# A hybrid attention layer on one core: attention steps of a tile spread over a slot and a half, with part of their elementwise work on GpSimd

## The chip, the cores and the metric

The kernel runs on one core of one Trainium2 chip. The metric is the device time of one execution in microseconds (us). Each core has a tensor engine (PE; PEld is its weight load), a vector engine (DVE), a scalar engine (ACT), GpSimd (POOL) and SyncE (SP), which here only issues DMAs. The engines run their own instruction streams in order and wait for one another through semaphores.

## What is computed

One inference step of one decoder layer: 2048 prompt positions and 8 x 4 sample positions, model width 1024. Its first part, on which the change bears, is cut here to what matters:

```
qa, ka, va, qb, kb, vb, ga, gb = split(x @ w_in)      # 1024 -> 5120
qa, ka, qb, kb = rope(...)
A:  8 query / 2 kv heads, window 128, learned sinks, in 128-blocks
B:  3 groups x 4 heads, (window, dilation) = (128,1), (512,4), (2048,16)
    keys of a block: the block before it and itself, masked to a band
    group 3 has one block per residue, so no block before it
ob = merge of the three groups by their softmax denominators
m  = sigmoid(ga) * (oa @ w_br_a) + sigmoid(gb) * (ob @ w_br_b);  m @ w_o
```

Samples do the same against cached keys and values. A gated ConvFFN and two layer norms follow. All is fp32 in and out; matmuls take each operand as a high part (rounded to the tensor engine's fp32r) and a low part (the rest), so a product takes three matmuls.

## The kernel before

Phase 1 is the input projection with the attention in it; phases 2 and 3 (merge, W_o, ConvFFN) aren't touched. Phase 1 runs in *slots*. A slot takes one tile of 128 rows (M) through the four weight units of its *kind*: B0, B1, B2 (q, k, v of one group and 256 gate columns), A, then G (gates alone). A kind has 16 tiles and, at i == 16, one *sample slot* for the 32 sample rows; the order of tiles is natural for B0 and A, strided by 4 for B1 and by 16 for B2. B1's tiles have a block before them except every fourth, B2's never have.

In a slot (`slot`), each of the four units goes through 8 blocks of k in two halves: 8 *steps* of 12 matmuls of 128x256 (8 of them in a sample slot). I name steps 0 to 7; step 2u + kh is unit u, half kh. After each step the code calls `adv`, which moves each waiting generator of `self.jobs` by one yield: this is where the attention of the tile before is interleaved. Steps also take two pieces of weight splitting for the next kind (`adv_w`, paced) and two times a slot a piece of the sample scores (`adv_bg`). Halves of the projection's output land in two PSUM buffers (`pd`); the first half's `evac` (the rope of q, for B of q and k) is called late, after step 5 in B and step 4 in A, the second half's (v, gate) at the slot's end. After step 1 (units 0 done), `prep` loads the next cos/sin and x and makes the next tile's `xs`: the high part on ACT, the low part on DVE (on GpSimd in A).

`attn_b` of a tile, by steps of the slot after its own: 0 transposes q, splits it, transposes k, splits it; 1 splits v; 2 scores (`qk`) and softmax (`softmax_pair`: per head a fused add-mask and maximum on DVE with its accumulator read, then nm = -scale x maximum on DVE, then the exponential with its sum on ACT); 5 and 6 transpose the two halves of P (`transpose_p`: PE, high part on ACT, low part on DVE); 7 and step 0 of the next slot multiply with the values and add the parts (`both`: ACT copies one half of the partitions, DVE adds; GpSimd adds the two products). `adv` takes the newest job first. `attn_a` has two rounds of scores (r = 0, 1; heads in pairs) whose four pairs' softmax, transposes and values are dealt out over ten steps singly. `sample_scores` multiplies a cached block of keys with broadcast queries (L797) and sums it (L800), both on DVE, in one piece.

PSUM tiles: psS 2 (scores), psT 3 (transposes, second value tile), psO 1 (values). All SBUF scratch of 128x512 comes from one ring of 10 (`buf`).

## Time and profile before

| what | us |
|---|---|
| median of 3 runs | 3261.59 (3256.7 to 3264.81) |
| the profiled execution | 3259.99, its span 3258.2 |
| PE, PEld busy | 3175.0 (97%), 2907.4 (89%) |
| DVE, ACT, POOL busy | 1947.6 (60%), 1397.0 (43%), 565.5 (17%) |
| dense projection matmuls L379 | 1001.1 busy, 7680 of them |
| mean granted PE clock | 0.994 |

PE's time is the sum of its pipelined matmuls as modelled, so that 97% says that it is hardly ever without one, not that it is at its peak. In the timeline a row is a run of alike instructions: its start, how long it lasts from the first's begin to the last's end, and in brackets how long the engine stood idle ahead of it and which instruction released it. Since matmuls overlap, the start of the next row tells more than the length.

### The profile page before, as it was taken

How to read it: one execution, taken by the hardware profiler on the slowest of the kernel's cores; microseconds unless marked ns; L12 is line 12 of the kernel's file. 1: busy time of each engine (PE TensorE's matmuls, PEld its weight loads, DVE VectorE, ACT ScalarE, POOL GpSimd, SP SyncE). 2: the span in 40 equal slices, each digit the busy share in tenths (PEclk: the TensorE clock that was granted, in tenths of full speed). 3: DMA queues.
4: the chain of work that ended last, by engine and by line, in shares of the span. 5: the costliest groups of instructions: out<-in, count | busy, mean ns of one | idle time of the engine just before them, and what ended most of it. 6: DMA issues, size and time to landing. Idle time of an engine off the chain costs nothing.

```text
span 3258.2 us, 56718 instructions
## 1 busy us (share of the span) xinstructions
PE 3175.0 (97%) x21839; PEld 2907.4 (89%) x21839; DVE 1947.6 (60%) x4030; ACT 1397.0 (43%) x3097; POOL 565.5 (17%) x671
## 2 busy tenths in 40 slices
PE   8999999999999899899999999999999999999999
PEld 8998999999899899788877988888888888999998
DVE  5667877877887632577765444564446444574446
ACT  6666656665666533412224243342243332342332
POOL 2112112223121200255540000030002100030001
PEclk9999999999999999999999999999999999999999
DMA  3113212412221343876744323443334423443231
GB/s 116 56 47 95 82 31 86 121 63 89 79 57 38 91 131 98 227 194 175 187 131 140 121 84 101 127 142 91 95 100 120 139 86 101 120 138 91 69 95 57
DMA packets 480036, 343.02 MB, mean 105 GB/s; under 512 B 113938, under 2 KB 435564, under 8 KB 479766
## 3 DMA queue, kind: packets, MB, share of 16 engines
q1 hardware_dynamic: 462390, 290.78, 31.5%
q0 software_dynamic: 17232, 48.56, 4.8%
q8 instruction: 172, 2.82, 0.4%
q14 instruction: 98, 0.80, 0.1%
q10 hardware_dynamic: 144, 0.07, 0.0%
HBM read 279.71 MB, written 59.59 MB: 104 GB/s over the span
## 4 chain that ended last, share of the span: by engine, by line
PE 58%; issue 2%; DMA 2%; DVE 1%; SPq 0%; ACT 0%; POOL 0%; DVEq 0%; POOLq 0%; ACTq 0%
PE psu L1392 31%; PE psdn L1070 14%; PE psw L1070 5%; PE psb L1070 4%; PE psd L379 2%; PE psdf L1070 1%; DMA oa<-d_oa 1%; PE pst L1234 0%; PE pso L964 0%; PE pst L1269 0%; DMA ob<-d_ob 0%; DMA ga<-d_gate 0%; DMA b<-in_w_o 0%; SPq L1126 0%; DMA b<-in_w_br_b 0%
## 5 line engine op out<-in xcount | busy, mean ns | idle before, releaser
L1392 PE MATMUL psu<-h,w 128*128 128x512 f32 (+1 forms) x5280 | 1013.6, 354 | 2.2 <-ACT h L41 2.0
L379 PE MATMUL psd<-w,xs 128*128 128x256 f32 x7680 | 1001.1, 285 | 8.7 <-ACT w L41 4.0
L1392 PEld LDWEIGHTS psu<-h,w 128*128 128x128 f32 x5280 | 861.2, 188 | 149.0 <-ACT h L41 3.4
L379 PEld LDWEIGHTS psd<-w,xs 128*128 128x128 f32 x7680 | 945.7, 190 | 12.9 <-ACT w L41 4.4
L1070 PE MATMUL psdn<-w,gt 128*128 128x256 f32 (+1 forms) x4008 | 474.9, 279 | 2.2 <-DVE y L1443 2.2
L1070 PEld LDWEIGHTS psdn<-w,gt 128*128 128x128 f32 (+1 forms) x4008 | 472.2, 186 | 5.3 <-DVE y L1443 4.5
L42 DVE TENSOR_TENSOR w<-b,w 128x512 fp32r<-128x512 f32 (+1 forms) x613 | 403.7, 717 | 21.4 <-ACT w L41 20.4
L41 ACT ACTIVATE w<-b 128x512 fp32r<-128x512 f32 x636 | 346.5, 607 | 127.4 <-PE psdn L1070 64.2
L1403 ACT ACTIVATE ext<-psu 128x512 f32<-128x512 f32 (+1 forms) x110 | 56.3, 512 | 452.2 <-PE psu L1392 452.1
L1416 DVE SCALAR_TENSOR_TENSOR ac<-ext,cw,ac 128x512 f32<-128x512 f32 (+1 forms) x88 | 71.1, 808 | 286.9 <-ACT ac L1415 286.9
L1443 DVE SCALAR_TENSOR_TENSOR y<-y,psdn 128x256 f32<-128x256 f32 x176 | 73.2, 420 | 274.2 <-PE psdn L1070 270.4
L1070 PE MATMUL psw<-WO,mT 128*128 128x512 f32 (+1 forms) x800 | 189.4, 395 | 0.9 <-DVE mT L42 0.9
L1070 PEld LDWEIGHTS psw<-WO,mT 128*128 128x128 f32 (+1 forms) x800 | 148.5, 186 | 38.9 <-DVE mT L42 1.1
L1412 POOL COPY mix<-ext 128x2 f32<-128x2 f32 x66 | 13.0, 196 | 926.5 <-ACT ext L1403 906.4
L42 DVE TENSOR_TENSOR xs<-R,xs 128x1024 fp32r<-128x1024 f32 x64 | 104.8, 1638 | 114.9 <-ACT xs L41 114.8
L1070 PE MATMUL psb<-w,oT 128*128 128x512 f32 (+1 forms) x600 | 147.6, 404 | 7.7 <-ACT b L449 5.0
L41 ACT ACTIVATE gt<-ac 128x512 fp32r<-128x512 f32 x110 | 58.3, 549 | 222.2 <-DVE ac L1423 162.7
L1070 PEld LDWEIGHTS psb<-w,oT 128*128 128x128 f32 (+1 forms) x600 | 112.4, 190 | 36.3 <-ACT b L449 5.7
L552 ACT ACTIVATE P<-P,nm 128x256 f32<-128x256 f32 (+1 forms) x192 | 86.4, 451 | 123.1 <-issue 87.4
L42 DVE TENSOR_TENSOR PT<-pst,PT 128x512 fp32r<-128x512 f32 (+1 forms) x160 | 96.2, 608 | 66.6 <-ACT PT L41 66.0
L662 POOL TENSOR_TENSOR b<-b 64x256 f32<-64x256 f32 x96 | 71.3, 742 | 337.4 <-DVE b L571 337.4
L41 ACT ACTIVATE xs<-R 128x1024 fp32r<-128x1024 f32 x80 | 116.2, 1452 | 0.9 <-ACT b L756 0.4
(257 smaller groups left out, 3679.1 us busy)
## 6 DMA issues: line engine op xcount, KB each, us to landing
b<-in_w_up SPq DMA_DIRECT2D x352, 256.0 KB, 3.9
b<-in_w_down SPq DMA_DIRECT2D x160, 256.0 KB, 3.4
b<-in_w_in SPq DMA_DIRECT2D x80, 256.0 KB, 4.1
b<-in_x_prompt SPq DMA_DIRECT2D x64, 256.0 KB, 4.0
b<-in_cache_b SPq DMA_DIRECT2D x64, 256.0 KB, 3.3
ga<-d_gate SPq DMA_DIRECT2D x32, 512.0 KB, 5.4
b<-d_q SPq DMA_DIRECT2D x48, 256.0 KB, 3.9
d_gate<-b SPq DMA_DIRECT2D x64, 128.0 KB, 1.9
```

Of the source, the lines that this page charges most:

```text
L41: self.nc.scalar.activation(hi, src, AF.Copy)
L42: (eng or self.nc.vector).tensor_tensor(lo, src, hi.bitcast(F32), ALU.subtract)
L379: nc.tensor.matmul(dst, lhsT=l, rhs=r[:, k, :], start=(k == 0 and q == 0), stop=(k == 7 and q == len(ops) - 1))
L552: nc.scalar.activation(P[:, x, :nk], P[:, x, :nk], AF.Exp, bias=nm[:, c:c + 1], scale=SCALE, accum_out=den[:, c:c + 1])
L662: nc.gpsimd.tensor_tensor(o[:, :, 0], o[:, :, 0], o[:, :, 1], ALU.add)
L1070: self.nc.tensor.matmul(ps[:x.shape[1]], lhsT=x, rhs=w, start=(first and q == 0), stop=(last and q == len(ops) - 1))
L1392: nc.tensor.matmul(ps[:, :b1 - b0], lhsT=w[:, k, c0:c0 + 128], rhs=h[:, x, k, b0:b1], start=(k == 0 and q == 0), stop=(k == 7 and q == 2))
L1403: nc.scalar.activation(ext[:, 2 + b0:2 + e1], ps[:, 0:e1 - b0], AF.Copy)
L1412: nc.gpsimd.tensor_copy(carry[:, j, :], ext[:, W:W + 2])
L1416: nc.vector.scalar_tensor_tensor(ac[:, :L], ext[:, 1:1 + L], cw[:, 1, j:j + 1], ac[:, :L], ALU.mult, ALU.add)
L1443: nc.vector.scalar_tensor_tensor(y[x][:M, cs], y[x][:M, cs], ALPHA if first else 1.0, ps[:M], ALU.mult, ALU.add)
```

## The change

- `adv` takes the oldest job first; what jobs hand to `self.late` runs behind all jobs of that step.
- `prep` runs at the slot's begin, ahead of step 0 (in B0's first slot after step 3). xs's low part goes to GpSimd in B1, B2 and A.
- The first half's rope comes after step 4 in B too. q, k and v of a tile share one buffer `qkv`, so that B's rope of q and k is three instructions of 512 columns and not five.
- `attn_b`: step 0 transposes q and k into one PSUM tile, all high parts ahead of all low ones (`split_qk`); 2 splits v; 3 scores and softmax; then, in the slot after, 0 transposes both halves of P, 2 multiplies both with the values, and `sum_b` adds behind the other jobs of that step.
- `attn_a`: 0 as before with `split_qk`; 3 the first scores; 5 both transposes and the second scores; 7 the first values; in the slot after 0 transposes and 2 values. The output goes out by round, not by kv head (two DMAs a round).
- nm is made on ACT.
- `sample_scores`: the product is made on GpSimd, its sum on DVE one piece later.
- Sample slots (but G's) call `adv` after steps 0, 1, 3 and 7 only.

The core of the diff:

```diff
     def adv(self):
-        for j in self.jobs[::-1]:
+        for j in list(self.jobs):
...
+        while self.late:
+            self.late.pop()()
...
-                        return self.make_xs(nextp[0][2], kind == "A")
+                        return self.make_xs(nextp[0][2], kind != "B0" and kind != "G")
...
-        evac_at = (2, 1) if kind[0] == "B" else (2, 0)
+        evac_at = (2, 0)
...
+        if kind != "B0" or i > 0:
+            out = prep()
         for half in range(2):
...
-                    self.adv()
+                    if not smp or kind == "G" or (u, kh) in ((0, 0), (0, 1), (1, 1), (3, 1)):
+                        self.adv()
...
-                self.rope([(q[:, 0:256].rearrange("p (h d) -> p h d", d=64), 0, 4),
-                           (kv[:, 0:256].rearrange("p (h d) -> p h d", d=64), 4, 8)], ps, cs, 128, 8)
+                self.rope([(t[:, 256:768].rearrange("p (h d) -> p h d", d=64), 0, 8)], ps, cs, 128, 8)
...
-        nc.vector.tensor_scalar(nm[:, csl], m[:, csl], -SCALE, None, ALU.mult)
+        nc.scalar.activation(nm[:, csl], m[:, csl], AF.Copy, scale=-SCALE)
...
+    def split_qk(self, q3, k3, cur):
+        qT, q_lo = self.split_q(q3)
+        k_lo = self.split_k(k3, cur)
+        q_lo()
+        k_lo()
+        return qT
...
         Ps = [self.softmax_pair(sps[x], nk, mask, md[:, 0:4], nm, md[:, 4:8], (x, 2 + x)) for x in range(2)]
         nc.gpsimd.dma_start(self.d_md[g, rows, :], md)
+        for _ in range(5):
+            yield
+        PTs = [self.transpose_p(P, [(c, b) for c in range(2) for b in range(nb)]) for P in Ps]
+        yield
+        yield
...
+        self.late.append(lambda: self.sum_b(g, i, tiles))
...
         sps = scores(0)
+        Ps = [softmax(0, x, sps) for x in range(2)]
         yield
         yield
+        PTs = [trans(P) for P in Ps]
         sps = scores(1)
+        Ps = [softmax(1, x, sps) for x in range(2)]
+        yield
+        yield
+        values(0, PTs)
+        yield
+        PTs = [trans(P) for P in Ps]
+        yield
+        yield
+        values(1, PTs)
...
+            if done is not None:
+                total(*done)
...
-            nc.vector.tensor_tensor(q3, Kv, q3, ALU.mult)
+            nc.gpsimd.tensor_tensor(q3, Kv, q3, ALU.mult)
+            done = (b, th, qb)
```

How this moves instructions shows at three places. PE in a B1 slot before, from the dense steps 2 to 4 on (L379 dense, L562 transposes of P, L659 values, L630 and L634 transposes of q and k of the next tile):

```order
L379 MATMUL psd<-w,xs 128x256 x36
L562 MATMUL pst<-idn,P 128x128 x4
L379 MATMUL psd<-w,xs 128x256 x12
L562 MATMUL pst<-idn,P 128x128 x4
L379 MATMUL psd<-w,xs 128x256 x12
L659 MATMUL pso<-PT,vr 128x256 x4
L379 MATMUL psd<-w,xs 128x256 x12
L630 MATMUL pst<-idn,q 128x128 x2
L634 MATMUL pst<-idn,kv 128x128 x2
L659 MATMUL pso<-PT,vr 128x256 x4
L379 MATMUL psd<-w,xs 128x256 x24
```

and after, from the dense steps 4 to 7 and 0 on (L383 dense, L566 P, L647 q and k, L673 values):

```order
L383 MATMUL psd<-w,xs 128x256 x60
L566 MATMUL pst<-idn,P 128x128 x8
L647 MATMUL pst<-idn,qkv 128x128 x4
L383 MATMUL psd<-w,xs 128x256 x24
L673 MATMUL pso<-PT,vr 128x256 x8
L383 MATMUL psd<-w,xs 128x256 x12
```

Sixty dense matmuls now follow the scores in one run, and two steps stand between P's transposes and the values.

PE in an A slot before, behind the first scores (L619 is their last matmul, L713 values, L562 the transposes of the first pair's P, L617 the second scores):

```order
L619 MATMUL pss<-kL_382,qT 128x256
L713 MATMUL pso<-PT,vr 128x256 x4
L379 MATMUL psd<-w,xs 128x256 x12
L713 MATMUL pso<-PT,vr 128x256 x4
L379 MATMUL psd<-w,xs 128x256 x12
L562 MATMUL pst<-idn,P 128x128 x4
L617 MATMUL pss<-kH_379,qT 128x256
```

and after (L636 the last of the first scores, L634 the first of the second ones):

```order
L636 MATMUL pss<-kL_408,qT 128x256
L383 MATMUL psd<-w,xs 128x256 x24
L566 MATMUL pst<-idn,P 128x128 x8
L634 MATMUL pss<-kH_405,qT 128x256
L634 MATMUL pss<-kH_406,qT 128x256
```

Both pairs' P are now transposed ahead of the second scores; before, the second pair's followed in the next slot.

DVE in the sample slot between B0 and B1 before (L546 maxima of the last tile, L550 nm, L42 lows of the next kind's weights w and of P, L495 the samples' first half):

```order
L546 ISA P,md<-pss,mk 128x256
L546 ISA md 128x1
L550 TENSOR_SCALAR nm<-md 128x2
L42 TENSOR_TENSOR w<-b,w 128x512 x3
L42 TENSOR_TENSOR PT<-pst,PT 128x512
L495 TENSOR_TENSOR b<-psd,b 32x512
```

and after, some instructions later in the same slot (L431 and L438 are the samples' rope, L550 is now the maxima):

```order
L431 TENSOR_TENSOR b<-b,css 32x512
L438 TENSOR_TENSOR sq<-sq,b 32x256
L438 TENSOR_TENSOR b<-b 32x256
L42 TENSOR_TENSOR w<-b,w 128x512 x5
L550 ISA P,md<-pss,mk 128x256
L550 ISA md 128x1
```

The last tile's maxima stood ahead of the weights' lows and now stand behind five of them, and behind them come the samples' second half and six more lows.

More of the change, by code (lines that the diff above doesn't have):

```diff
@@ L219, in phase1 @@
             units += [self.next_unit(pool=True) for _ in range(2)]
-            self.jobs = []
+            self.jobs, self.late = [], []
             self.vprev = None
@@ L388, in slot @@
                         self.adv_bg()
-                if u == (1 if kind[0] == "B" and i == 0 else 0):
+                if u == 1 and kind == "B0" and i == 0:
                     out = prep()
-                    if kind == "G" and i == 14:
-                        rp.close()
-                        self.phase2_weights()
+                if u == 0 and kind == "G" and i == 14:
+                    rp.close()
+                    self.phase2_weights()
                 after_unit(u)
@@ L460, in evac @@
             cs = self.cs = self.css.pop(0)
-            q = self.at1.tile([128, 512], F32, tag="q", name="q")
-            kv = self.at1.tile([128, 512], F32, tag="kv", name="kv")
-            self.q, self.kv = q, kv
+            t = self.at1.tile([128, 1024], F32, tag="qkv", name="qkv")
+            q = t[:, 0:512] if kind == "A" else t[:, 256:512]
+            self.q, self.kv = q, t[:, 512:1024]
             if kind == "A":
@@ L589, in split_q, with lo @@
             nc.scalar.activation(qT[x][here, :n], q3[here], AF.Copy)
-        for x, here, there in self.HALF:
-            nc.vector.tensor_tensor(qT[x][there, :n], q3[here], qT[x][here, :n].bitcast(F32), ALU.subtract)
-        return qT
+        def lo():
+            for x, here, there in self.HALF:
+                nc.vector.tensor_tensor(qT[x][there, :n], q3[here], qT[x][here, :n].bitcast(F32), ALU.subtract)
+        return qT, lo
     def split_k(self, k3, cur):
@@ L606, in split_k, with lo @@
             nc.scalar.activation(self.kH[x][there, :n, cur], k3[here], AF.Copy)
-        for x, here, there in self.HALF:
-            nc.vector.tensor_tensor(self.kL[x][here, :n, cur], k3[here], self.kH[x][here, :n, cur].bitcast(F32), ALU.subtract)
+        def lo():
+            for x, here, there in self.HALF:
+                nc.vector.tensor_tensor(self.kL[x][here, :n, cur], k3[here], self.kH[x][here, :n, cur].bitcast(F32), ALU.subtract)
+        return lo
     def qk(self, qT, sl, nk, pairs):
@@ L628, in attn_b @@
         ps = self.psT.tile([128, 512], F32, tag="t", name="pst")
-        for p in range(2):
-            nc.tensor.transpose(ps[:, p * 128:(p + 1) * 128], q[:, p * 128:(p + 1) * 128], self.idn)
-        qT = self.split_q(ps[:, 0:256].rearrange("p (r t) -> p r t", r=2))
-        ps = self.psO.tile([128, 512], F32, tag="o", name="pst")
-        for p in range(2):
-            nc.tensor.transpose(ps[:, p * 128:(p + 1) * 128], kv[:, p * 128:(p + 1) * 128], self.idn)
-        self.split_k(ps[:, 0:256].rearrange("p (r t) -> p r t", r=2), i % 2)
+        for p in range(4):
+            nc.tensor.transpose(ps[:, p * 128:(p + 1) * 128], (q, kv)[p // 2][:, p % 2 * 128:(p % 2 + 1) * 128], self.idn)
+        ps = ps.rearrange("p (r t) -> p r t", r=4)
+        qT = self.split_qk(ps[:, 0:2], ps[:, 2:4], i % 2)
+        yield
         yield
@@ L638, in attn_b @@
         vprev, self.vprev = self.vprev, v
+        vs = [v] if nb == 1 else ([v, vprev] if swap else [vprev, v])
         yield
@@ L660, in attn_b, with sum_b @@
                                      rhs=PTs[x][:, :, k:k + 128], start=(b == 0), stop=(b == nb - 1))
+        self.late.append(lambda: self.sum_b(g, i, tiles))
+    def sum_b(self, g, i, tiles):
+        nc = self.nc
+        O = self.buf()
+        for x, ops in enumerate(tiles):
             o = self.both(O, ops, x).rearrange("p (c s t) -> p c s t", c=2, s=2)
@@ L708, in trans, with values @@
             return self.transpose_p(P, [(y, b) for b in range(nb) for y in range(2)])
-        def values(r, x, PT):
-            for b in range(nb):
-                for q in range(2):
-                    nc.tensor.matmul(ops[:, r * 256:(r + 1) * 256], lhsT=vs[b][:, x], rhs=PT[:, q, b * 256:(b + 1) * 256],
-                                     start=(b == 0 and q == 0), stop=(b == nb - 1 and q == 1))
-        def out(x):
-            o = self.both(O, ops, x)
-            nc.gpsimd.dma_start(self.d_oa[x * 256:(x + 1) * 256, rows].rearrange("(h d) t -> d h t", h=4),
-                                o.rearrange("p (h t) -> p h t", h=4))
+        def values(r, PTs):
+            ops = self.psO.tile([128, 512], F32, tag="o", name="pso")
+            for x in range(2):
+                for b in range(nb):
+                    for q in range(2):
+                        nc.tensor.matmul(ops[:, x * 256:(x + 1) * 256], lhsT=vs[b][:, x],
+                                         rhs=PTs[x][:, q, b * 256:(b + 1) * 256],
+                                         start=(b == 0 and q == 0), stop=(b == nb - 1 and q == 1))
+            o = self.both(self.buf(), ops, r)
+            for x in range(2):
+                h0 = (4 * x + 2 * r) * 64
+                nc.gpsimd.dma_start(self.d_oa[h0:h0 + 128, rows].rearrange("(y d) t -> d y t", y=2),
+                                    o[:, x * 256:(x + 1) * 256].rearrange("p (y t) -> p y t", y=2))
```

43 lines of the change are left out of this document (11 added, 32 removed).

## The prediction

> **What bounds the kernel now.** I read the page first, then busy times of each engine over the stretches of the input projection, then the tensor engine's timeline inside single slots, then the groups of the instructions that the change moves. A slot is one 128-row tile going through the four weight units of its kind (96 dense matmuls, 12 to a step, 8 steps), with the attention of the tile before interleaved between steps. All that the change touches lies in these slots; behind about 1119 us only the preparation of the next tile moves, by two steps. The stretches below are, in order: eleven slots of kind B0, the change of kind to B1 (its sample slot and first tile), fifteen slots of B1, the change to B2, fifteen slots of B2, the change to A, fourteen slots of A, the change to G. Columns: length, then busy time of PE, PEld, DVE, ACT, POOL, the granted clock, DMA share, GB/s.
>
> ```profile
> 75.36:245.43 170.07, 170.07 (x1455) 169.68 (x1454) 106.76 (x287) 105.70 (x264) 30.17 (x44) 1.00 0.18 54
> 259.46:292.54 33.08, 27.83 (x210) 25.97 (x209) 28.16 (x50) 21.13 (x46) 12.54 (x13) 0.95 0.38 114
> 292.54:523.05 230.51, 220.42 (x1822) 213.58 (x1821) 172.51 (x421) 137.50 (x332) 40.53 (x60) 1.00 0.20 59
> 523.05:555.13 32.08, 27.71 (x203) 26.24 (x202) 27.27 (x48) 20.68 (x46) 12.83 (x14) 0.89 0.39 118
> 555.13:769.20 214.07, 208.61 (x1736) 203.60 (x1735) 159.18 (x421) 129.38 (x343) 46.44 (x72) 1.00 0.29 88
> 769.20:813.85 44.65, 41.16 (x315) 39.47 (x314) 34.98 (x81) 26.69 (x76) 17.45 (x15) 0.92 0.31 96
> 813.85:1081.42 267.57, 260.15 (x2075) 244.61 (x2073) 214.08 (x546) 163.05 (x486) 51.24 (x42) 1.00 0.22 60
> 1081.42:1119.30 37.88, 30.01 (x233) 27.20 (x232) 27.43 (x61) 25.64 (x65) 10.81 (x11) 1.00 0.36 100
> ```
>
> In B0 PE never stops (170.07 of 170.07), so B0 can't gain. In B1, B2 and A it stands idle 10.1, 5.5 and 7.4 us, in the four changes of kind 5.3, 4.4, 3.5 and 7.9 us. DVE is at 75 to 80% in B1 and A, and at 85% in the changes. So PE bounds, with stops that others cause. How dear a stop is shows in one B1 slot, PE alone:
>
> ```profile
> 447.08 0.38 PE L630 MATMUL pst<-idn,q 128*128 128x128 f32 x2
> ...
> 447.99 3.00 PE L379 MATMUL psd<-w,xs 128*128 128x256 f32 x24
> 450.83 0.40 PE L617 MATMUL pss<-kH,qT 128*128 128x256 f32 x2
> ...
> 451.78 4.42 PE L379 MATMUL psd<-w,xs 128*128 128x256 f32 x36
> 456.65 0.93 PE L562 MATMUL pst<-idn,P 128*128 128x128 f32 x4 [0.45 <-ACT P L552]
> 457.34 1.66 PE L379 MATMUL psd<-w,xs 128*128 128x256 f32 x12
> 458.84 0.60 PE L562 MATMUL pst<-idn,P 128*128 128x128 f32 x4
> 459.19 1.66 PE L379 MATMUL psd<-w,xs 128*128 128x256 f32 x12
> ...
> 462.58 0.38 PE L630 MATMUL pst<-idn,q 128*128 128x128 f32 x2
> ```
>
> 24 dense matmuls take 450.83 - 447.99 = 2.84 us, 0.118 each. So the 36 that begin at 451.78 hand over at 456.04; the transposes of P begin at 456.65, 0.61 late, and take 0.69 until the next dense one where the second four take 0.35. The stop that reads 0.45 costs 0.95. The slot lasts 15.50; without it **14.55**, the length at which PE alone sets a B slot with a previous block.
>
> In B2 (no previous block) the same is seen smaller:
>
> ```profile
> 717.46 4.47 PE L379 MATMUL psd<-w,xs 128*128 128x256 f32 x36
> 722.10 0.71 PE L562 MATMUL pst<-idn,P 128*128 128x128 f32 x2 [0.17 <-ACT P L552]
> 722.57 1.66 PE L379 MATMUL psd<-w,xs 128*128 128x256 f32 x12
> 724.07 0.38 PE L562 MATMUL pst<-idn,P 128*128 128x128 f32 x2
> 724.21 1.07 PE L379 MATMUL psd<-w,xs 128*128 128x256 f32 x7
> ```
>
> The dense run should end at 717.46 + 4.26 = 721.72; the transposes start 0.38 later and take 0.47 instead of 0.14: 0.71 in all. A B2 slot is 214.07 / 15 = 14.27 long on average, the one shown 14.32, so its floor is **13.6**.
>
> **The change part by part.** The sum is made against the profiled execution (3259.99 us, of them 3258.2 in the span); the median of the runs is 1.6 above it. A difference under 0.3% (10 us) can't be told from none.
>
> *B1 and B2.* The new order gives every hand-over more dense steps: P has from step 3 to step 0 of the next slot (five steps, was two and three), its low parts two steps, the first scores three. What remains to be shown is that the other engines keep up with 14.55. Their instructions by these rows (min, median, max ns; the last pair of the groups with mean):
>
> ```profile
> L41 ACT ACTIVATE xs<-R x14: 2025/2070/2100, 310.1 to 511.9; 128x1024 fp32r<-128x1024 f32 x14
> L42 DVE TENSOR_TENSOR xs<-R,xs x14: 1961/2032/2048, 312.2 to 514.0; 128x1024 fp32r<-128x1024 f32 x14
> ```
>
> ```profile
> L41 ACT ACTIVATE PT<-pst x30: 358/576/602, 302.0 to 520.5; 128x512 fp32r<-128x512 f32 x22, 128x256 fp32r<-128x256 f32 x8
> L42 DVE TENSOR_TENSOR PT<-pst,PT x30: 415/684/693, 302.4 to 522.2; 128x512 fp32r<-128x512 f32 x22, 128x256 fp32r<-128x256 f32 x8
> ```
>
> ```profile
> L604 ACT ACTIVATE kH<-pst x30: 377/379/382, 307.6 to 524.7; 64x256 fp32r<-64x256 f32 x30
> ```
>
> ```profile
> L662 POOL TENSOR_TENSOR b<-b 64x256 f32<-64x256 f32 x96 | 71.3, 742 | 337.4 <-DVE b L571 337.4
> L1221 POOL TENSOR_TENSOR m<-ga 128x512 f32<-128x512 f32 x32 | 45.9, 1436 | 49.2 <-DVE ga L1215 41.4 <-ACT w L41 7.6
> ...
> L42 POOL TENSOR_TENSOR xs<-R,xs 128x1024 fp32r<-128x1024 f32 x16 | 38.8, 2422 | 6.7 <-ACT xs L41 5.5
> ```
>
> Count from a slot's start. ACT: gate copy 0.4, high part of xs 2.07, two highs of P at 0.6 end at 3.7; two highs of q and four of k, 0.38 each, end at 6.0. DVE: lows of P end at 4.4, of q and k (estimate: as long as their highs) by 6.4. PE: dense 1.42, eight P transposes 0.70, four of q and k 0.35, dense 2.84: it wants P's lows for the values at 5.3 (0.9 to spare), and the lows of q and k at 5.3 + 0.95 + 1.42 = 7.7 (1.3 to spare). The scores end at 8.65; DVE comes to them at 9.6, behind two sums and a reduction (0.7 each, P's row of 512 columns); maxima to 11.4 (0.91 a pair, a row below), exponentials to 12.7; P is wanted at 14.55 + 1.4. The rope, three instructions of 0.7, now stands behind the maxima and ends at 13.5, wanted at 16.7: 3.2 to spare. So PE should not stop. In B2 both sides shrink together (0.8 and 0.6 to spare).
>
> What DVE loses: xs's low part (2.03) and one product per sample step, for GpSimd. GpSimd gains them: 2.42 for contiguous xs; here R is read with a step of 4 or 16 elements, which no GpSimd row shows, so between 2.42 and twice that (4.84); I take 3, nearer the only row. Products: 1.44 each by the row of the same shape. With two additions of 0.74 and about 1.9 us of DMA issues that is 9.3 us of 14.55 (11.2 at the upper end). The additions and the two products are queued behind xs, and one product behind d_md, which waits for the exponentials at 13; the sums of the products come a sample step later on DVE, so nobody waits. As the cover is whole, I cost it at nothing. Loads that go two steps earlier with the slot's preparation (cos and sin, x, all on SP) and A's output in four pieces instead of two (GpSimd's queue) have no reader within the slot: nothing. In B0, xs stays on DVE ahead of P's lows; at the prices of the rows with a step they would come 1.0 late, +15 over the stage; its xs is contiguous, so shorter, and PE has x's transposes ahead: I take nothing, and the 15 stays for the range.
>
> B1: eleven intervals at 14.55 and four (no previous block) at 13.6 make 214.5, against 230.5: **-16.0**. B2: 15 x 13.6 = 204.0 against 214.1: **-10.1**.
>
> *A.* Its floor is B's with one more set of scores (450.83 to 451.78: 0.95), eight more transposes (0.70), eight more value matmuls (8 x 0.118 = 0.95) and one of k (0.09): 17.24. The new order has two stops. Second scores and both sets of first transposes stand together, two dense steps (2.84) behind the first scores. Rows, first GpSimd's and DVE's timeline in one slot, then the groups of ACT's exponentials and DVE's nm:
>
> ```profile
> 955.37 2.39 POOL L42 TENSOR_TENSOR xs<-R,xs 128x1024 fp32r<-128x1024 f32 x1
> ```
>
> ```profile
> 955.47 0.47 DVE L695 CUSTOM_DVE_ANT_0 P<-pss,mk,sk 128x256 f32<-128x256 f32 x1
> ...
> 956.38 1.40 DVE L698 TENSOR_SCALAR nm<-m 128x2 f32<-128x2 f32 x1
> ```
>
> ```profile
> L700 ACT ACTIVATE P<-P,nm x110: 492/506/516, 822.0 to 1078.0; 128x257 f32<-128x257 f32 x110
> ```
>
> ```profile
> L698 DVE TENSOR_SCALAR nm<-m x64: 168/170/1891, 804.5 to 1104.8; 128x2 f32<-128x2 f32 x64
> ```
>
> Two maxima take 0.91 on DVE (955.47 to 956.38), nm on ACT between DVE's 0.17 (last row) and the 0.38 of a 256-wide copy, I take 0.2, two exponentials 1.1 with the read of their sums. The second P is ready 0.9 + 0.2 + 1.1 + 0.4 + 1.1 = 3.8 after the scores with hand-over gaps; PE has its first four transposes done at 2.84 + 0.35 = 3.2. It stops 0.6, by the B1 slot's rule about 0.8 in all. k's transpose waits for its rope, which follows the sums: 0.3. So 18.34 a slot; fourteen make 256.8 against 267.6: **-10.8**.
>
> The negated maxima leave DVE. In the rows above nm ends at 957.78, when GpSimd's xs ends (957.76): an instruction of 0.17 took 1.40. The Trainium skill (SBUF — State Buffer, Who interferes with whom) has it that such a VectorE instruction and one of GpSimd exclude each other on a shared port, and these rows agree; it adds that a VectorE instruction with two inputs in SBUF is held as well by a GpSimd instruction that reads SBUF, which no row of the steady slots shows. That part speaks against the change; what it could cost is the third rival.
>
> *Changes of kind.* DVE is busy 28.2 of 33.1 us there. It loses xs's low (2.03) and two nm (0.34), so -2.4 if it sets the pace. Against this the last tile's maxima now stand behind five lows of weights, and on ACT the exponentials stand ahead of the next weights: up to two maxima and two exponentials, 0.9 + 0.2 + 1.1 twice less what overlaps, +3.8 at most; if all idle goes, -5.3. I take -1.5 each, nearest to DVE's row, for three changes: **-4.5**. To G, where DVE is busy only 27.4 of 37.9 and PE stops 7.9, two thirds: **-5.0**. The clock of 0.95, 0.89 and 0.92 there stays as it is.
>
> Sum -46.4. I give back 0.2 us for each of 44 slots, since hand-overs with 0.6 to 1.3 us to spare by rows of another order will not all hold: +8.8. That leaves -37.6: 3222.4 for a profiled execution, **3224** beside the median.
>
> **The rivals.** *Stops only move (0.22).* PE's hidden losses stay and half of its visible idle goes elsewhere: for it speaks that DVE and ACT stay strict queues and P's lows have 0.9 to spare. The idle of B1 and B2 and a third of A's go: 10.1 + 5.5 + 2.5 = 18, so 3243.
>
> *Changes of kind run clean (0.13).* No allowance, and the low clock goes too: (1 - 0.95) x 33.1 + (1 - 0.89) x 32.1 + (1 - 0.92) x 44.7 = 8.8. Then 46.4 + 8.8 = 55, so 3206. For it: fewer attention steps in the sample slot. Against: weights still pass ACT and DVE one after another.
>
> *GpSimd holds the rope, slower (0.10).* Place: the rope's last addition in each B1 and B2 slot. If the strided xs costs 4.84 and runs late, it, an addition and a product follow each other there (4.84 + 0.74 + 1.44 = 7.0), and DVE stands for that long if it is held through all of them, as nm was held through one. By the rule of the page above this addition is of the held kind. The rope has 3.2 to spare and P's lows 0.9: from a hold of 4.1 on it costs PE, here 2.9 a slot. Thirty slots: +87, and the B gain of 26.1 is gone: 3261.6 + 87 - 11.5 = 3337; at a hold of 5 us it is +27 - 11.5, 3277. Against it: GpSimd is idle a third of the slot and its queue has no reason to bunch there.
>
> **How the numbers follow.** The forecast has 0.55. Range: from the clean rival, 3206, to 3250, past the rival whose stops only move; outside lies the slower one with 0.10 and a little at each end. Faster by over 0.3% (below 3251.8): the forecast 0.55, clean 0.13, and 0.19 of the moved stops, 0.87. Within 0.3%: 0.03 of those and 0.02 of the slower rival, 0.05. Slower: 0.08.
>
> **What would show it.** Right: B1 intervals of 14.5 to 14.8 and B2 of 13.6 to 13.8 between the first transposes of q, with no idle before values or scores; A near 18.3, with PE's only stops at the second four transposes of P and at k's; nm gone from DVE and no long one on ACT; B0 unchanged at 15.46. Wrong: PE waiting for low parts of P before the values, for DVE's rope before the first dense step of a slot, or for GpSimd's xs; a strided xs on GpSimd above 4.84 us; or changes of kind longer than 33 us, with ACT waiting for DVE's maxima while weights stand behind them.

## The result and the profile after

| | before | after |
|---|---|---|
| median of the runs, us | 3261.14 (4 runs) | 3226.89 (3222.75 to 3229.41, 4 runs) |
| ratio | 1 | 0.9895, 95% interval 0.9882 to 0.9907 |
| profiled execution, its span | 3259.99, 3258.2 | 3227.46, 3225.7 |

The forecast was 3224, between 3206 and 3250. To compare stage by stage I cut the span at the first dense matmul of a slot. A *change* runs from a kind's sample slot to the third tile of the next kind, a *steady* stretch from there to the kind's own sample slot (fourteen slots). The kernel after, in that order from the change to B1 to the change to G; columns: start and end, length, then busy time of PE, PEld, DVE, ACT, POOL, the granted clock, DMA share, GB/s:

```profile
256.14:304.33 48.19, 41.84 (x318) 40.25 (x317) 31.22 (x62) 29.08 (x69) 20.08 (x16) 0.93 0.30 87
304.33:504.18 199.85, 199.85 (x1706) 199.85 (x1705) 121.05 (x310) 132.51 (x339) 102.20 (x89) 1.00 0.23 66
504.18:552.38 48.20, 41.40 (x319) 39.08 (x317) 31.18 (x62) 29.18 (x70) 20.61 (x17) 0.96 0.31 95
552.38:744.03 191.65, 191.65 (x1627) 191.45 (x1625) 111.50 (x310) 124.22 (x350) 107.32 (x100) 1.00 0.31 94
744.03:791.73 47.70, 41.17 (x320) 39.01 (x319) 32.61 (x74) 28.73 (x84) 18.85 (x15) 0.96 0.31 90
791.73:1047.01 255.28, 251.87 (x2080) 244.07 (x2079) 180.14 (x478) 173.84 (x545) 89.08 (x86) 1.00 0.24 63
1047.01:1095.58 48.57, 44.16 (x333) 41.27 (x332) 30.05 (x58) 27.46 (x70) 14.20 (x17) 0.93 0.39 99
```

PE is busy for 199.85 of 199.85 us in B1 and 191.65 of 191.65 in B2: no stop is left there that the profile shows. The first row shows the other side: a change lasts 48 us, with PE idle for 6.4 of them. Before, the same stretches were, in this order, 45.39, 217.26, 45.21, 200.94, 44.17, 268.05 and 50.13 us; the granted clock in its four changes was 0.96, 0.92, 0.92 and 1.00.

A B1 slot after, PE alone:

```profile
433.84 1.04 PE L566 MATMUL pst<-idn,P 128*128 128x128 f32 x8
434.71 0.60 PE L647 MATMUL pst<-idn,qkv 128*128 128x128 f32 x4
435.07 3.10 PE L383 MATMUL psd<-w,xs 128*128 128x256 f32 x24
438.00 1.09 PE L673 MATMUL pso<-PT,vr 128*128 128x256 f32 x8
...
441.29 7.26 PE L383 MATMUL psd<-w,xs 128*128 128x256 f32 x60
448.39 0.82 PE L566 MATMUL pst<-idn,P 128*128 128x128 f32 x6
```

From one set of P transposes to the next are 448.39 - 433.84 = 14.55 us, the floor that the prediction read from before, with no bracket in any row. An A slot after keeps one stop, at the second pair's P:

```profile
965.33 3.01 PE L383 MATMUL psd<-w,xs 128*128 128x256 f32 x24
968.17 0.93 PE L566 MATMUL pst<-idn,P 128*128 128x128 f32 x5
969.27 0.55 PE L566 MATMUL pst<-idn,P 128*128 128x128 f32 x3 [0.17 <-ACT P L721]
969.57 0.48 PE L634 MATMUL pss<-kH,qT 128*128 128x256 f32 x2
```

Eight transposes take 969.57 - 968.17 = 1.40 here, where the eight of a B slot take 0.87.

### The profile page after: what moved, and what is told of

It reads as the page before. It is cut to its first block, busy times and chain, and to the rows that moved or that the text cites. A ratio compares the mean times of both kernels' runs of the same rounds, so it can differ in the third digit from the quotient of the medians.

```text
span 3225.7 us, 56679 instructions
## 1 busy us (share of the span) xinstructions
PE 3157.8 (98%) x21839; PEld 2909.1 (90%) x21839; DVE 1813.1 (56%) x3694; ACT 1419.3 (44%) x3257; POOL 747.1 (23%) x783
## 4 chain that ended last, share of the span: by engine, by line
PE 67%; issue 6%; DVE 4%; ACT 3%; DMA 2%; POOL 1%; SPq 0%; DVEq 0%; POOLq 0%; ACTq 0%
PE psu L1411 31%; PE psdn L1089 14%; PE psd L383 8%; PE psw L1089 5%; PE psb L1089 4%; PE psdf L1089 1%; ACT P L721 1%; DVE w L42 1%; PE pst L566 1%; DMA oa<-d_oa 1%; PE pso L736 1%; DVE P L716 0%; PE pst L1253 0%; DVE b L575 0%; PE pss L636 0%
## 5 line engine op out<-in xcount | busy, mean ns | idle before, releaser
L383 PE MATMUL psd<-w,xs 128*128 128x256 f32 x7680 | 978.1, 284 | 21.1 <-DVE w L42 7.1
L383 PEld LDWEIGHTS psd<-w,xs 128*128 128x128 f32 x7680 | 935.9, 190 | 28.2 <-ACT w L41 10.2
L42 DVE TENSOR_TENSOR w<-b,w 128x512 fp32r<-128x512 f32 (+1 forms) x613 | 406.8, 722 | 19.2 <-ACT w L41 18.1
L42 DVE TENSOR_TENSOR PT<-pst,PT 128x512 fp32r<-128x512 f32 (+1 forms) x160 | 91.5, 608 | 154.4 <-ACT PT L41 153.7
L42 POOL TENSOR_TENSOR xs<-R,xs 128x1024 fp32r<-128x1024 f32 x48 | 131.9, 2748 | 62.8 <-ACT xs L41 54.2
L42 DVE TENSOR_TENSOR xs<-R,xs 128x1024 fp32r<-128x1024 f32 x32 | 41.6, 1298 | 146.2 <-ACT xs L41 146.1
```

The costliest lines, as they stand in the source:

```text
L42: (eng or self.nc.vector).tensor_tensor(lo, src, hi.bitcast(F32), ALU.subtract)
L383: nc.tensor.matmul(dst, lhsT=l, rhs=r[:, k, :], start=(k == 0 and q == 0), stop=(k == 7 and q == len(ops) - 1))
```

## The experiments

All stages of all kernels, from their profiled executions. "to B0 s" is the span's start to B0's sample slot, "behind" what follows G's third tile; the medians of the runs are at the end. The kernel before was timed beside each set; it had 3258.8 to 3261.1.

```
kernel                 to B0 s  to B1   B1 st   to B2   B2 st    to A    A st    to G   behind  median
before                  259.46  45.39  217.26   45.21  200.94   44.17  268.05   50.13  2127.58  3261.14
after                   256.14  48.19  199.85   48.20  191.65   47.70  255.29   48.57  2130.10  3226.89
e1  all points          257.60  48.11  199.85   48.67  191.59   46.41  255.01   51.87  2124.48  3224.69
e2  xs low on DVE       254.26  47.32  200.97   47.31  192.91   47.71  255.28   48.55  2126.72  3222.17
e3  before, xs on POOL  258.93  44.53  209.54   44.54  194.94   44.15  268.44   50.10  2127.06  3243.98
e4  nm on DVE           255.46  48.90  200.01   48.03  192.53   47.47  273.25   48.36  2127.32  3242.67
e5  spread alone        255.80  47.31  200.89   47.31  192.90   47.73  262.76   48.56  2126.52  3230.69
e6  first xs late       256.88  45.28  199.89   45.57  191.61   47.70  255.01   48.58  2127.90  3219.22
e7  before, nm on ACT   258.97  46.70  218.53   45.44  202.22   44.37  251.67   49.82  2130.43  3249.93
e8  last tile packed    255.54  47.28  199.85   47.19  191.57   47.02  255.00   48.58  2123.75  3218.98
e9  e6 and the old A    256.23  45.28  199.88   45.62  191.56   48.06  250.28   52.07  2123.83  3214.91
e10 e9 and packed       255.79  46.24  199.85   47.79  191.57   47.26  250.33   52.27  2129.05  3218.12
e11 e9, four points     255.08  45.22  199.89   45.33  191.58   48.51  250.29   49.87  2125.40  3212.95
e12 e11, all in B2      255.48  45.48  199.85   45.75  191.47   46.18  250.25   49.82  2123.86  3209.92
```

The columns from "to B1" to "A st" repeat to some 0.4 us where two kernels don't differ; among the kernels with the new slot the first column and "behind" vary by 3.3 and 6.4 us, though their code is the same there, so a difference of a few us between medians is read from the stages.

**Fewer points in the sample slots.** Why the changes had grown I first put down to what the prediction had named: the last tile's maxima behind five lows of weights.

```diff
-                    if not smp or kind == "G" or (u, kh) in ((0, 0), (0, 1), (1, 1), (3, 1)):
-                        self.adv()
+                    self.adv()
```

> Undoes one part: the attention is driven at all eight steps of the sample slots again, as before, and not at four. Theory (with only four points the last tile's scores come at the sample slot's end, its maxima stand behind five lows of weights on DVE, and ACT stands at their negation with the next weights queued behind it): the three changes of kind, which in the changed kernel grew by 3.4 to 3.6 us each, get 2 to 3.5 us shorter each, ACT's idle of 6.7 us ahead of the negated maxima shrinks below 3 us, steady slots stay at 14.54, 13.69 and 18.2; in all 6 to 10 us less, 3217 to 3221. Rival one (the growth comes from nm on ACT or from GpSimd's holds): changes of kind within 1 us of the changed kernel, 3227. Rival two (the four points were worth what they cost, the whole attention in a sample slot that has only 64 matmuls stops PE more): changes of kind longer, 3230 to 3240.

3224.69, ratio to before 0.9891 (0.9876 to 0.9906). The theory falls: ACT's wait ahead of the negation shrank from 6.74 to 2.67, as expected, and the changes to B1 and B2 stayed (48.11, 48.67); the one to A got 1.3 shorter. In the kernel after, that wait does cost PE a stop, 2.04 at 278.83 (shown below with e6): the samples' second half stands behind the exponentials on ACT. In e1 this stop is gone and others come in its place; PE's rows in the change to B1:

```profile
272.12 1.69 PE L383 MATMUL psd<-w,xs 128*128 128x256 f32 x12 [3.18 <-DVE b L498]
...
281.27 2.07 PE L672 MATMUL pso<-PT,vr 128*128 128x256 f32 x8 [2.51 <-DVE PT L42]
```

The first waits for the first half of the samples' output, which now stands behind the exponentials on ACT, the second for P's lows. For the change to G the second rival holds: with all points it is 51.87, with four 48.57.

**The low half of xs, and the spread alone.** In e2 xs's low half returns to DVE, in e5 the sample products as well; e3 is the kernel before with only the low half on GpSimd.

```diff
# e2 and e5 (and the reverse of it, in the kernel before, is e3)
-                        return self.make_xs(nextp[0][2], kind != "B0" and kind != "G")
+                        return self.make_xs(nextp[0][2], kind == "A")
# e5 besides
-            nc.gpsimd.tensor_tensor(q3, Kv, q3, ALU.mult)
+            nc.vector.tensor_tensor(q3, Kv, q3, ALU.mult)
```

> Undoes one part: the low half of xs in the slots of B1 and B2 is on DVE again (2.03 us) and not on GpSimd. Theory (the gain of the steady slots is from the wider hand-overs, and the offload gives the room that they need): DVE has the low half ahead of P's low halves only where it is issued first; P's lows then end about 2 us later, at 6.4 us of the slot where PE wants them at 5.3, so a B1 slot gets 0.6 to 1.2 us longer (15.1 to 15.7) and a B2 slot 0.3 to 1.0, in all 12 to 30 us more, 3239 to 3257. Rival (the spread alone carries the gain and DVE has room for 2 us): B1 stays within 0.1 of 14.54, B2 within 0.1 of 13.69, 3227.

> The changed kernel with nothing handed to GpSimd: the low half of xs in B1 and B2 and the sample products are on DVE again; the spread, the split at a slot's begin and the negation on ACT stay. Theory (the spread carries the steady gain of B1 and B2, the offload is a substitute and not needed beside it): B1 slots 14.5 to 14.65, B2 slots 13.7 to 13.95, A 18.2 to 18.6 (a product of 0.7 us stands ahead of the maxima in some slots), in all 3221 to 3232. Rival (DVE, now with 5 us more of work in a B slot, becomes late for P's low halves): B1 at 14.9 or more and B2 at 14.0 or more, 3236 to 3255.

> The kernel before with one part of the change alone: the low half of xs of B1 and B2 goes to GpSimd. Theory (the spread carries the gain): the P transposes still stand two dense steps behind the maxima; the offload takes 2 us from DVE ahead of the maxima, but these wait for the scores, not for DVE alone, so the slots of B1 and B2 gain at most a third of what the whole change gave: 0 to 0.4 us a slot of 1.0, 0 to 12 us in all, 3249 to 3261. Rival (the offload carries the gain, and the spread is decoration): B1 at 14.5 to 14.7 and B2 at 13.7, 22 to 28 us less, 3233 to 3239.

e2: 3222.17, ratio 0.9885 (0.9870 to 0.9900). The rival is right: most B1 slots with a previous block stay at 14.49 to 14.55 (one in three or so takes 14.77), B2's are 13.8 against 13.7. Rows of DVE in a B1 slot of e2:

```profile
433.04 2.06 DVE L42 TENSOR_TENSOR xs<-R,xs 128x1024 fp32r<-128x1024 f32 x1 [3.22 <-ACT xs L41]
435.01 1.28 DVE L42 TENSOR_TENSOR PT<-pst,PT 128x512 fp32r<-128x512 f32 x2
```

P's first lows are there at 435.65, half of the pair; the values begin at 436.06 without a stop. The second half has until the first four values are done. e5: 3230.69 (0.9896 to 0.9926 around 0.9911), with B as in e2, so the new order without the offload gives what B gains. What is worse is A: 262.76 against 255.28 in e2. In its slot a product of 0.68 on DVE (at 819.47) now stands ahead of the maxima (820.18), and PE's stops at P's transposes add up to 5.3 in the stage, against 2.3 in e2.

e3: 3243.98 (0.9932 to 0.9965 around 0.9948), 15.7 less than before, between both theories. The offload alone does give 7.7 in B1 and 6.0 in B2. Why not more, PE's groups over the fourteen slots of B1 say (behind the second bar stands PE's idle time ahead of them and what ended most of it). Before:

```profile
L562 PE MATMUL pst<-idn,P 128*128 128x128 f32 x100 | 18.7, 285 | 3.5 <-ACT P L552 2.7
L634 PE MATMUL pst<-idn,kv 128*128 128x128 f32 x28 | 5.8, 290 | 6.6 <-DVE b L571 6.6
```

In e3:

```profile
L562 PE MATMUL pst<-idn,P 128*128 128x128 f32 x100 | 15.5, 272 | 0.0
L634 PE MATMUL pst<-idn,kv 128*128 128x128 f32 x28 | 6.0, 296 | 6.1 <-DVE b L571 6.1
```

Before, B1 had two stops, and the larger was not at P: k's transposes write to the PSUM tile of the values (`psO`) and wait until DVE's sum (L571) has read it; in one slot the sum begins at 401.06, behind a sample product and its reduction, and PE goes on at 401.79. In B2 it was 4.3 at k and 0.9 at P. The offload takes P's stop away and leaves 6.1 and 2.4 at k's; the new order, which puts k's transposes into q's PSUM tile, has neither, in e5 too. So for P's stop the spread and the offload are substitutes, for k's they are not; how much of the new order's gain is the shared tile's and how much the wider hand-overs', no run takes apart. On top of the new order the offload gives 1.1 and 1.3 in the steady stretches and costs 0.9 in each of the changes to B1 and B2. In e3 another thing shows, GpSimd and DVE side by side:

```profile
448.17 2.91 POOL L42 TENSOR_TENSOR xs<-R,xs 128x1024 fp32r<-128x1024 f32 x1
448.30 2.80 DVE L550 TENSOR_SCALAR nm<-md 128x2 f32<-128x2 f32 x1
```

An instruction that otherwise takes 0.17 is held until GpSimd is done.

**The negation.** e4 returns it to DVE, e7 moves it to ACT in the kernel before.

```diff
# e4 (e7 is the reverse, in the kernel before)
-        nc.scalar.activation(nm[:, csl], m[:, csl], AF.Copy, scale=-SCALE)
+        nc.vector.tensor_scalar(nm[:, csl], m[:, csl], -SCALE, None, ALU.mult)
...
-            nc.scalar.activation(nm[:, c:c + 2], m[:, c:c + 2], AF.Copy, scale=-SCALE)
+            nc.vector.tensor_scalar(nm[:, c:c + 2], m[:, c:c + 2], -SCALE, None, ALU.mult)
```

> Undoes one part: the negated maxima are made on DVE again and not on ACT, in B0 to B2 and in A. Theory (ACT stands still in the changes of kind because of the maxima themselves, wherever they are negated): changes of kind within 0.7 us of the changed kernel; in steady slots nm on DVE is held now and then by GpSimd's xs (up to 1.9 us) but the wider hand-over hides it: slots of B within 0.1, slots of A 0 to 0.3 longer, 3225 to 3233. Rival (nm on ACT makes the changes of kind long): these get 2 to 3.5 us shorter each, 3217 to 3221.

> The kernel before with one part of the change alone: the negated maxima are made on ACT. Theory (on DVE they are held by GpSimd's instructions, and the exponentials, P and PE wait for that): A slots fall from 19.02 to 18.2 to 18.7, 5 to 12 us in all; in B1 and B2, where the next P is waited for as well, 0 to 0.4 a slot; in all 3243 to 3254. Rival (the negation only matters with the new order of A, where two sets of P stand together; the old order has other stops): A slots within 0.2 of 19.02, 3256 to 3262.

e4: 3242.67, ratio 0.9945 (0.9930 to 0.9960): 16 us lost, outside of both expectations. The changes don't move by more than 0.7, so the rival falls; A alone goes from 255.29 to 273.25. Its slot, GpSimd, DVE and PE together:

```profile
981.45 2.99 PE L383 MATMUL psd<-w,xs 128*128 128x256 f32 x24
982.55 1.30 POOL L817 TENSOR_TENSOR b<-b 128x512 f32<-128x512 f32 x1
982.67 1.22 DVE L719 TENSOR_SCALAR nm<-m 128x2 f32<-128x2 f32 x1
...
984.64 0.33 PE L566 MATMUL pst<-idn,P 128*128 128x128 f32 x1 [0.20 <-ACT P L721]
...
986.66 0.48 PE L634 MATMUL pss<-kH,qT 128*128 128x256 f32 x2
```

The sample product, now on GpSimd, holds nm, for 1.22 in all; P comes that much later, and the eight transposes take 986.66 - 984.29 = 2.4 (24 dense matmuls from 981.45 on end at 984.29) instead of 1.40. Over the stage PE's stops at P's transposes are 13.3, against 2.3 in the kernel after.

e7: 3249.93, ratio 0.9966 (0.9951 to 0.9980). A falls from 268.05 to **251.67**, further than in the whole change. An A slot of e7, from one set of q transposes to the next, lasts 18.00, and ACT's nm takes 0.20 beside GpSimd's xs (PE, GpSimd and ACT together):

```profile
943.38 0.60 PE L676 MATMUL pst<-idn,q 128*128 128x128 f32 x4
...
950.00 2.40 POOL L42 TENSOR_TENSOR xs<-R,xs 128x1024 fp32r<-128x1024 f32 x1
...
951.01 0.20 ACT L698 ACTIVATE nm<-m 128x2 f32<-128x2 f32 x1 [1.00 <-DVE m L695]
...
961.38 0.60 PE L676 MATMUL pst<-idn,q 128*128 128x128 f32 x4
```

So in A the negation is worth 16.4 in the old order and 18.0 in the new one, and the new order by itself (with its products on GpSimd) costs 3.6 to 5.2. In B1 and B2 e7 loses 1.3 each. What grows there is the stop at k's transposes, from 6.6 to 8.5 in B1 and from 4.3 to 6.1 in B2, while the one at P shrinks by 0.6 each; that the sum comes later because the negation lengthens ACT's queue ahead of its copy isn't shown.

**Where the changes grew.** Two causes were left: that the next tile's xs is made ahead of the first step even in a kind's first slot, and that the last tile's attention reaches into that slot.

```diff
# e6
-        if kind != "B0" or i > 0:
+        if i > 0 or kind == "G":
             out = prep()
...
-                if u == 1 and kind == "B0" and i == 0:
+                if i == 0 and u == (1 if kind[0] == "B" else 0) and kind != "G":
                     out = prep()
# e8
-                    if not smp or kind == "G" or (u, kh) in ((0, 0), (0, 1), (1, 1), (3, 1)):
+                    if not smp or kind != "A" or (u, kh) in ((0, 0), (0, 1), (1, 1), (3, 1)):
...
-        for _ in range(5):
+        for _ in range(5 if i < 15 else 3):
             yield
```

> Undoes one part in four slots alone: in the first slot of B0, B1, B2 and A the next tile's xs is made after the unit where it stood before (the second of a B kind, the first of A) and not ahead of the first step. Theory (in the changes of kind the high half of xs, 2.07 us on ACT, and its low half, 2.9 us on GpSimd, now stand ahead of P's halves and of the next weights, which PE waits for): the stretches from a kind's sample slot to its third tile, 48.2, 48.2 and 47.7 us in the changed kernel and 45.4, 45.2 and 44.2 before, get 1.5 to 3 us shorter each; in all 4 to 8 us less, 3218 to 3223. Rival (they are long because the last tile's attention now reaches into the first slot of the next kind): within 0.7 us of the changed kernel each, 3225 to 3229.

> In the sample slots of the B kinds the attention is driven at all eight steps, and the last tile of a B kind has three steps between scores and P instead of five, so that its P is made in the sample slot, as before; A is as in the changed kernel. Theory (the changes of kind are long because the last tile's attention reaches into the first slot of the next kind, where its P halves stand behind the sums and weights): the changes to B1, B2 and A get 2 to 3 us shorter each, 6 to 9 us in all, 3218 to 3221. Rival (they are long because xs is made ahead of the first step there): changes within 0.8 us of the changed kernel, 3225 to 3229.

e6: 3219.22, ratio 0.9876 (0.9862 to 0.9891). The changes to B1 and B2 are 45.28 and 45.57, what they were before the change; the one to A doesn't move (47.70). e6 moves the slot's loads with xs; that it is xs, the rows say. The kernel after first, in the first slot of B1:

```profile
274.94 0.20 ACT L554 ACTIVATE nm<-md 128x2 f32<-128x2 f32 x1 [6.74 <-DVE md L550]
...
278.83 0.49 PE L383 MATMUL psd<-w,xs 128*128 128x256 f32 x2 [2.04 <-DVE b L499]
278.92 2.08 ACT L41 ACTIVATE xs<-R 128x1024 fp32r<-128x1024 f32 x1
...
280.91 2.17 ACT L41 ACTIVATE w<-b 128x512 fp32r<-128x512 f32 x4
281.08 2.90 POOL L42 TENSOR_TENSOR xs<-R,xs 128x1024 fp32r<-128x1024 f32 x1 [0.33 <-ACT xs L41]
281.56 5.88 DVE L42 TENSOR_TENSOR w<-b,w 128x512 fp32r<-128x512 f32 x4 [1.95 <-ACT w L41]
...
284.59 0.97 PE L383 MATMUL psd<-w,xs 128*128 128x256 f32 x6 [1.06 <-DVE w L42]
286.28 0.97 PE L383 MATMUL psd<-w,xs 128*128 128x256 f32 x6 [0.72 <-DVE w L42]
```

The same place in e6:

```profile
275.69 0.20 ACT L554 ACTIVATE nm<-md 128x2 f32<-128x2 f32 x1 [6.75 <-DVE md L550]
...
278.63 3.21 ACT L41 ACTIVATE w<-b 128x512 fp32r<-128x512 f32 x6
279.58 0.65 PE L383 MATMUL psd<-w,xs 128*128 128x256 f32 x2 [2.07 <-DVE b L499]
279.68 5.87 DVE L42 TENSOR_TENSOR w<-b,w 128x512 fp32r<-128x512 f32 x6
...
283.13 2.11 ACT L41 ACTIVATE xs<-R 128x1024 fp32r<-128x1024 f32 x1
283.70 3.08 PE L383 MATMUL psd<-w,xs 128*128 128x256 f32 x24
```

After, xs's high half stands between the weights' highs on ACT: DVE gets nothing for 1.95, then its first low, held until GpSimd's xs is done (283.98), takes 2.98, so that four lows take 5.88 where six take 5.87 in e6, and PE stops twice more for them. The granted clock is not the difference: 0.93 and 0.96 in the changes to B1 and B2 after, 0.92 and 0.96 in e6. The wait that the prediction had named, ACT ahead of the negation, is the same in both, 6.74 and 6.75, and so is the stop that it costs PE, 2.04 and 2.07.

e8: 3218.98, ratio 0.9875 (0.9860 to 0.9890), in the theory's range, but not for its reason alone: the changes are 0.9, 1.0 and 0.7 shorter, not 2 to 3; 6.4 us of its span's difference lie behind G, where the code is the same.

**Put together.** e9 is e6 with the whole of A as before but for the negation; e10 packs the last tile besides; e11 has four points in A's sample slot and A's first xs after the second unit; e12 all points in B2's sample slot.

```diff
# e9, to e6: attn_a of the kernel before with nm on ACT (not shown), and
-        if i > 0 or kind == "G":
+        if kind != "A" and i > 0 or kind == "G":
             out = prep()
...
-        for j in list(self.jobs):
+        for j in self.jobs[::-1] if self.rev else list(self.jobs):
...
+        self.rev = kind in ("A", "G")
...
+                    if not smp or kind in ("A", "G") or (u, kh) in ((0, 0), (0, 1), (1, 1), (3, 1)):
...
+                if kind == "A" and u == 0 or i == 0 and u == 1 and kind[0] == "B":
                     out = prep()
# e11, to e9 (e12: with kind in ("B2", "G") in the first line)
-                    if not smp or kind in ("A", "G") or (u, kh) in ((0, 0), (0, 1), (1, 1), (3, 1)):
+                    if not smp or kind == "G" or (u, kh) in ((0, 0), (0, 1), (1, 1), (3, 1)):
...
-                if kind == "A" and u == 0 or i == 0 and u == 1 and kind[0] == "B":
+                if kind != "G" and u == (1 if i == 0 else 0) and (i == 0 or kind == "A"):
```

> The kernel of the run in which the first tile's xs is made late, and besides the whole of A as in the kernel before (its attention in one-set steps, the newest tile first, xs after the first unit, all points in its sample slot), with the negation on ACT kept. Theory (A's gain is the negation's alone, and its new order costs something, since the kernel before with the negation on ACT had A slots of 17.98 against 18.21): A's fifteen slots 250 to 253 us against 255.0, the change to A 44.5 to 46.5 against 47.7, the change to G 49.5 to 50.2 against 48.6; in all 2 to 6 us less than 3219.2, 3213 to 3217. Rival (the old order of A needs DVE as the old slots left it, with the products there): A's slots within 1.5 us of 255.0, 3218 to 3223.

> The same and besides the last tile of a B kind packed (three steps between scores and P, all points in its sample slot). Theory (both lengthen the changes of kind, but by the same queue: with xs late there is little left for the packing to remove): the changes to B1 and B2 at 44.5 to 45.5, the change to A at 44.3 to 45.5; in all 0 to 3 us less than without the packing. Rival (two separate costs that add up): 0.9 a change less than without, 42.5 to 44.5 in the changes to B1 and B2, 3 us or more less in all. Rival (packing puts the last tile's steps back on the weights): 1 us or more longer a change.

> The fastest kernel so far (the changed kernel's B kinds, the old A with the negation on ACT, first tiles' xs late) with two more edits: A's sample slot has the four points of the changed kernel again, and A's first tile has its xs made after the second unit, as the B kinds' first tiles. Theory (with few points the last A tile's steps don't stop the short sample slot, which cost 3.5 us in the change to G; in the change to A the high half of xs stands ahead of P's halves): change to G 48.5 to 50.5 against 52.07, change to A 46.5 to 48 against 48.06, A's slots within 0.5 of 250.3; in all 1.5 to 5 us less than that kernel. Rival (the old A's twelve steps take up in G's first slots what they save in the sample slot): change to G 51.5 to 53, nothing gained.

> The same, with B2's sample slot at all eight points. Theory (without a previous block the last B2 tile has half the transposes, scores and values, so its maxima can come before the weights' lows): change to A 0.5 to 1.5 us shorter than with four points, as it was 1.3 shorter in the changed kernel with all points; nothing else moves. Rival: within 0.4 us.

e9: 3214.91 (0.9849 to 0.9878 around 0.9864); A at 250.28, as the theory had it, 4.7 less than in e6. The change to A (48.06) and that to G (52.07) missed the expectation, both too long. e10: 3218.12 (0.9854 to 0.9887 around 0.9871): mostly the third branch, packing costs 1.0 and 2.2 in the changes to B1 and B2 once xs is late, though the change to A gets 0.8 shorter. e11: 3212.95 (0.9839 to 0.9867 around 0.9853): four points take 2.2 off the change to G; the later xs does nothing for the change to A. e12: **3209.92** (0.9835 to 0.9863 around 0.9849), the change to A 2.3 shorter, more than the 0.5 to 1.5 expected; the granted clock in it is 0.96 against 0.93 in e11, so part of the 2.3 may be the clock's. It beats the changed kernel: their intervals, 0.9835 to 0.9863 and 0.9882 to 0.9907, lie apart.

## Why the prediction was right, point by point

The sum was -37.6 against the profiled execution and came out at -32.5. By its terms:

| term | forecast | measured |
|---|---|---|
| B0 | 0 | -3.3 |
| B1, B2 | -16.0, -10.1 | -17.4, -9.3 (fourteen slots each) |
| A | -10.8 | -12.8 |
| three changes of kind | -4.5 | +2.8, +3.0, +3.5: **+9.3** |
| to G | -5.0 | -1.6 |
| given back in 44 slots | +8.8 | 0 |
| behind G | 0 | +2.5 |

*B1 and B2: right in size, one of two stops seen.* Slots of 14.55 and 13.7 are the forecast's floors of 14.55 and 13.6, and the new order is what reaches them (e5). The slot that the prediction read has its stop at P, with k's transposes free; in eight of the fourteen slots of B1 PE stopped at k's, 6.6 in all against 2.7 at P, and the prediction doesn't name that stop. As its floor leaves out every stop, the sum came out all the same. The cover held; it holds even with xs's low half left on DVE, which the prediction's own count (P's lows 0.9 to spare, xs 2.03) would not have allowed. The rows of e2 show why: the first half of P's lows, which the values start with, is ready at 435.65, and PE comes to them at 436.06.

*A: the size nearly right, the ground wrong.* The prediction had 18.34 a slot as the sum of the new order's floor (17.24) and two stops (1.1), and took the negation as a term within. Measured are 18.21 in most slots (18.24 on average), with one stop, and e4 and e7 show that all of the gain is the negation's. It had the row in hand: nm at 1.40 instead of 0.17. In each of the fourteen slots before one nm is held like that, for 1.40 to 1.89; the hold of 1.23, less what was hidden, fits the 1.02 that e7 gains per slot (19.02 to 18.00). The floor was too low: the old order without a visible stop still takes 18.00. Of the two stops forecast the one at k's transposes didn't come.

*Changes of kind: the step that failed.* "I take -1.5 each, nearest to DVE's row" had the wrong sign. Its own sign of being wrong was there: cut as the prediction cut it, from the sample slot to the next tile's transposes of q, the change to B1 takes 292.70 - 256.14 = 36.6, over 33, with ACT waiting for the maxima. The mechanism named against it (maxima behind five lows, up to +3.8) is in the trace and costs PE a stop of 2.0, but it isn't what the changes grew by: e1 takes it away and gets stops of 3.18 and 2.51 for it, e6 leaves it and gains 2.9 and 2.6, nearly all of the growth. What made the changes to B1 and B2 longer was priced at nothing: with the slot's preparation go not only loads but xs, and in a B kind's first slot by four steps, ahead of weights that PE waits for. For the change to A this isn't the cause (e6, e11); all points in B2's sample slot give 1.3 (e1) to 2.3 (e12) of its 3.5, the rest stays open.

*To G.* Four points are right here (3.3 by e1), but most of what the sample slot saves comes back in G's first slot: the one went from 18.65 to 10.96, the other from 20.09 to 26.22, where with all points (e1) they are 18.43 and 22.05. The granted clock of this change fell from 1.00 to 0.93, which no term of the forecast had.

*The allowance* of 8.8 had no ground: the clean slots give nothing back. It stood by chance for what the changes took, and so the total came out near: by luck, as the changes missed by 13.8. The difference behind G can't be told from its own variation: in kernels with the same code there that stretch lasted from 2123.75 to 2130.10. *B0* was 254.3 to 257.6 in the kernels with the new slot and 258.9 to 259.5 with the old one. Of its 3.3, 2.5 lie in its fourteen steady slots (216.16 to 213.69), 0.9 of them in the last one, where the kernel before had a stop of 0.36 at P; the stretch from which the prediction read that B0 can't gain ends at 245.43, before it. The rest I haven't taken apart.

*Rivals.* Stops that only move: no, in the steady slots they went. Changes that run clean: no, they grew. GpSimd holding the rope: xs does not in the steady slots, since it took 2.92 strided (2.40 contiguous, against 3 and 2.42 assumed) and was done before the rope. A sample product does: in 15 of the 42 steady slots of B1, B2 and A the rope's last addition takes 0.92 to 1.63 instead of 0.69. The longest, in B2:

```profile
563.52 1.28 POOL L817 TENSOR_TENSOR b<-b 128x512 f32<-128x512 f32 x1
563.72 1.63 DVE L438 TENSOR_TENSOR qkv<-qkv,b 128x512 f32<-128x512 f32 x1
```

PE doesn't stop for it in B1 and B2; the hold stays far below the 3.2 that the prediction had to spare. Where xs comes late it holds the rope too. In e12, in A's first slot:

```profile
766.15 2.40 POOL L42 TENSOR_TENSOR xs<-R,xs 128x1024 fp32r<-128x1024 f32 x1
...
766.95 2.15 DVE L439 TENSOR_TENSOR qkv<-qkv,b 128x512 f32<-128x512 f32 x1
```

The addition takes 2.15 instead of 0.69. The changed kernel has it in the change to G, where the samples' rope is held beside two weights' lows:

```profile
1057.21 3.20 DVE L431 TENSOR_TENSOR b<-b,css 32x512 f32<-32x512 f32 x1
1057.32 2.54 POOL L42 TENSOR_TENSOR w<-b,w 128x512 fp32r<-128x512 f32 x2
...
1061.78 1.45 PE L383 MATMUL psd<-w,xs 128*128 128x256 f32 x10 [2.00 <-DVE w L42]
```

0.68 became 3.20, and the weights' lows that PE waits for came that much later. The Trainium skill (SBUF — State Buffer, Who interferes with whom) says that a VectorE instruction with two inputs in SBUF contends with a GpSimd instruction that reads SBUF; no steady slot of before showed it, these rows of the rope do. P's lows, which read one input from PSUM, took 0.65 each beside xs (435.48 in the B1 slot, xs from 435.04 to 437.96): not held, as the same section has it.

## What to carry to other kernels

Before splitting a change's gain among its parts, look for the one row in the steady slot that is longer than its group's median and stands on the path: here a negation of two columns, held for 1.2 us, was worth 16 us of A, while the new order around it cost 3.6 to 5.2. Read a stage's stops from all of its slots, by what ended them, and not from one slot: here the one that was read had the smaller of two stops. A step that is moved ahead can cost nothing in the steady slots and much where another stream (the next weights) uses the same queues, 2.9 and 2.6 us here, so price it at the irregular places apart. Two remedies for the same stop don't add up: check each alone.

## What the runs showed of the hardware that was not expected

- The hold between DVE and GpSimd has no fine grain: a DVE instruction of 0.17 on 2 columns took 2.80 beside a GpSimd one of 2.91 (e3) and 1.22 beside one of 1.30 (e4). Of two additions of the same shape, the one beside GpSimd's xs took 2.15 (e12), a free one 0.69.
- It holds in both directions: in the change to B1 a GpSimd low of a weight took 3.06, while DVE made five of the same kind, against 1.27 alone:

```profile
267.34 1.27 POOL L42 TENSOR_TENSOR w<-b,w 128x512 fp32r<-128x512 f32 x1
...
270.05 4.18 DVE L42 TENSOR_TENSOR w<-b,w 128x512 fp32r<-128x512 f32 x5
...
270.62 3.06 POOL L42 TENSOR_TENSOR w<-b,w 128x512 fp32r<-128x512 f32 x1
```

- The maxima on DVE, whose mask comes from SBUF and whose scores come from PSUM, took 0.47 to 0.48 beside GpSimd's product as without it.
